# LayerNorm with GELU on one core: the last 128 rows as two half tiles, one of them on 15 DMA engines, and empty instructions ahead of two instruction streams

## The chip, the core and the metric

One NeuronCore of a Trainium2 chip. The metric is the device time of the whole kernel in microseconds (us). Every kernel below was run beside the kernel before on the same chip. "Span" is the time from the first to the last recorded instruction; the measured time of the same run is 1.8 to 2.0 us longer.

## The reference

```python
# x: (8, 1024, 2048) float32; gamma, beta: (2048,)
mean = np.mean(x, axis=-1, keepdims=True)
var = np.var(x, axis=-1, keepdims=True)
out = gamma * (x - mean) / np.sqrt(var + eps) + beta
return 0.5 * out * (1 + np.tanh(np.sqrt(2 / np.pi) * (out + 0.044715 * out ** 3)))
```

There are 8192 rows of 8 KB: 67.1 MB to read and 67.1 MB to write.

## The kernel before

The rows go through SBUF in 16 blocks of 512. A block is a tile of 128 partitions with 4 rows (32 KB) each, and there are 5 such slots. SyncE issues the loads, ScalarE the stores. A slot's next load waits until its store has landed.

```python
# SyncE
for b in range(B):
    s = slot(b)
    if stored(b):
        sy.wait_ge(s_store[s], stored(b))
    ...                                   # block 0: four loads of 1 MB, one for each q
    if b:
        sy.dma_start(out=xts[s], in_=xg[b]).then_inc(s_load[s], 16)
```

For each of the 64 tiles of 128 rows VectorE takes the statistics, GpSimd the power -1/2, ScalarE normalizes, VectorE multiplies by gamma, TensorE adds beta in PSUM by a matmul, and ScalarE applies GELU and issues the store: whole blocks, but the last block tile by tile.

```python
# ScalarE, after the GELU of tile q of block b
if by_row(b):                             # the last block
    ac.dma_start(out=og[b, :, q:q + 1], in_=xt[:, q:q + 1])._wait_ge(
        s_r, b + q + 1).then_inc(s_store[slot(b)], 16)
```

VectorE's stream is a prologue (block 0), a loop of 20 tiles that runs 3 times, and an end. ScalarE's stream is unrolled.

## Time and profile before

| | before |
|---|---|
| time, median of 6 runs | 319.69 us (319.23 to 320.06) |
| span of the profiled run | 317.8 us |
| DMA, mean over the span | 423 GB/s |
| busiest compute engine | VectorE, 83% |
| last store issued, last store landed | 305.32, 316.50 us |
| last packet of 14 DMA engines | 313.3 to 313.9 us |
| last packet of the other two | 316.06 us both |

The last two rows are not on the page. The trace holds a record of each DMA packet with queue, start, duration and size, but without its engine. The packets were strung into 16 chains, as the prediction tells, choosing the fit with the smallest sum of gaps; the last packet of each chain is the last of one engine. Two engines at the same point in time can swap names in it; a chain 2 us behind the rest cannot be mistaken. "Excess" is what a chain's data packets took beyond the usual duration of their size (1213 ns for 32 KB, 309 ns for 8 KB).

### The profile page before, as it was taken

What the parts mean: (1) busy time and instruction counts of PE and PEld (TensorE: products, weight loads), DVE (VectorE), ACT (ScalarE), POOL (GpSimd) and SP (SyncE); (2) the same over time, 40 slices, a digit from 0 to 9 for tenths busy, and PEclk for the clock granted to TensorE, in tenths of its full rate; (3) what the DMA queues carried; (4) which work ended last, traced back from release to release, by engine and by line L of the source; (5) the groups of instructions that cost most, each with busy time, mean ns of one, the idle gap of its engine ahead of it and who ended that gap; (6) DMA issues with size and microseconds to landing.
All of it is one profiled execution on the core that took longest, in us unless ns stands there. A gap on an engine that the chain in (4) does not pass through costs nothing.

```text
span 317.8 us, 2075 instructions
## 1 busy us (share of the span) xinstructions
PE 244.3 (77%) x520; PEld 57.1 (18%) x520; DVE 265.0 (83%) x514; ACT 253.9 (80%) x132; POOL 79.0 (25%) x73
## 2 busy tenths in 40 slices
PE   2769988888888898888877868598595895868810
PEld 1211222111212122211111111122121111112100
DVE  3499999999999999999969799696996969879500
ACT  2679999999999999999969779696995969968920
POOL 1033323232323231323213222231312213212000
DMA  7999999999999999999999999999999999999994
GB/s 291 438 462 396 459 396 445 412 454 404 458 400 459 422 437 445 412 450 408 458 417 441 437 421 454 404 458 412 450 433 425 450 408 450 408 458 421 437 404 206
DMA packets 5571, 134.27 MB, mean 423 GB/s; under 512 B 656, under 2 KB 704, under 8 KB 704
## 3 DMA queue, kind: packets, MB, share of 16 engines
q1 hardware_dynamic: 2736, 67.11, 49.4%
q10 hardware_dynamic: 2832, 67.13, 49.1%
q14 instruction: 3, 0.02, 0.0%
HBM read 67.13 MB, written 67.11 MB: 422 GB/s over the span
## 4 chain that ended last, share of the span: by engine, by line
DMA 44%; DVE 27%; ACT 19%; PE 3%; issue 2%; ACTq 1%; DVEq 0%; SPq 0%
DMA out_dram<-xt 27%; DVE sts L148 15%; DMA xt<-in_x_dram 15%; ACT yk L201 12%; DVE zg L164 9%; ACT xt L208 7%; PE ps L226 2%; DMA rows<-in_gamma_dram 2%; DVE mvs L157 2%; DVE nms L141 1%; ACTq L216 1%; DVE ves L158 1%; PE ps L243 1%; ACT g_t L197 1%; ACTq L211 0%
## 5 line engine op out<-in xcount | busy, mean ns | idle before, releaser
L148 DVE BATCH_NORM_STATS2 sts<-xt 128x6 f32<-128x512 f32 x256 | 163.5, 681 | 23.7 <-DMA xt<-in_x_dram 21.7
L201 ACT ACTIVATE yk<-xt,nms,rss 128x2048 bf16<-128x2048 f32 x64 | 134.1, 2095 | 41.7 <-DVE nms L141 41.2
L243 PE MATMUL ps<-zg,ident 128*128 128x512 bf16 x256 | 120.8, 627 | 50.9 <-DVE zg L164 50.9
L132 POOL TENSOR_TENSOR rss<-ves,mhalf 128x1 f32<-128x1 f32 x64 | 78.0, 1219 | 216.5 <-DVE ves L158 157.0
L239 PE MATMUL ps<-b_hl,ones_b 33*128 33x512 bf16 x256 | 120.6, 624 | 2.2 <-PEq L234 2.2
L208 ACT ACTIVATE xt<-ps 128x2048 f32<-128x2048 f32 x64 | 118.8, 1857 | 1.5 <-PE ps L243 1.5
L164 DVE TENSOR_TENSOR zg<-yk,g_t 128x2048 bf16<-128x2048 bf16 x64 | 78.0, 1218 | 5.0 <-ACT yk L201 3.0
L243 PEld LDWEIGHTS ps<-zg,ident 128*128 128x128 bf16 x256 | 27.6, 130 | 144.1 <-DVE zg L164 108.7
L239 PEld LDWEIGHTS ps<-b_hl,ones_b 33*128 33x128 bf16 x256 | 27.0, 127 | 92.1 <-issue 88.4
L157 DVE BATCH_NORM_AGGREGATE mvs<-sts 128x2 f32<-128x24 f32 x64 | 16.9, 264 | 2.2
L141 DVE TENSOR_SCALAR nms<-mvs,rss 128x1 f32<-128x1 f32 x64 | 12.6, 196 | 0.0
L226 PE MATMUL ps<-rows,ones 1*128 1x512 f32 x8 | 7.2, 1072 | 6.0 <-DMA rows<-in_gamma_dram 6.0
L158 DVE TENSOR_SCALAR ves<-mvs 128x1 f32<-128x1 f32 x64 | 9.8, 154 | 2.2
L194 ACT ACTIVATE b_hl<-rows 1x2048 bf16<-1x2048 f32 x1 | 1.9, 1909 | 4.9 <-DMA rows<-in_beta_dram 4.9
L226 PEld LDWEIGHTS ps<-rows,ones 1*128 1x128 f32 x8 | 2.5, 323 | 9.2 <-DMA rows<-in_gamma_dram 6.0
L172 DVE TENSOR_TENSOR b_hl<-rows,b_hl 1x2048 bf16<-1x2048 f32 x1 | 2.3, 2281 | 2.1 <-ACT b_hl L195 2.1
L197 ACT ACTIVATE g_t<-ps 128x2048 bf16<-128x2048 f32 x1 | 1.9, 1877 | 2.4 <-PE ps L226 2.4
L190 ACT ACT_TABLE_LOAD x1 | 1.3, 1283 | 0.9 <-SPq L106 0.9
L167 DVE MEMSET b_hl<- 33x1024 uint32 x1 | 0.9, 912 | 1.2 <-SPq L106 1.2
L195 ACT ACTIVATE b_hl<-rows 1x2048 bf16<-1x2048 f32 x1 | 1.9, 1908 | 0.0
L123 POOL MEMSET ones<- 65x128 f32 x1 | 0.2, 202 | 0.5 <-SPq L106 0.5
L127 POOL TENSOR_SCALAR_AFFINE_SELECT ident<-ident 128x128 bf16<-128x128 bf16 x1 | 0.3, 294 | 0.1
(7 smaller groups left out, 0.9 us busy)
## 6 DMA issues: line engine op xcount, KB each, us to landing
xt<-in_x_dram SPq DMA_DIRECT2D x15, 4096.0 KB, 24.3
out_dram<-xt ACTq DMA_DIRECT2D x15, 4096.0 KB, 37.0
xt<-in_x_dram SPq DMA_DIRECT2D x4, 1024.0 KB, 8.1
out_dram<-xt ACTq DMA_DIRECT2D x4, 1024.0 KB, 12.7
rows<-in_beta_dram ACTq DMA_DIRECT2D x2, 8.0 KB, 5.6
rows<-in_gamma_dram ACTq DMA_DIRECT2D x1, 8.0 KB, 5.0
```

The lines of the kernel that those rows point to most:

```text
L132: po.tensor_tensor(out=rss[:, c], in0=ves[:, c], in1=mhalf, op=ALU.pow)._wait_ge(s_a, k + 1).then_inc(s_q, 1)
L141: ve.tensor_scalar(out=nms[:, c], in0=mvs[:, q, 0:1], scalar1=rss[:, c], scalar2=-1.0, op0=ALU.mult, op1=ALU.mult)._wait_ge(s_q, count).th ...
L148: ins = ve.bn_stats(out=sts[:, q, j, :], in_=xr[:, j, :])
L157: ve.bn_aggr(out=mvs[:, q], in_=sts[:, q])._wait_ge(s_o, count + 1).then_inc(s_o, 1)
L158: ve.tensor_scalar(out=ves[:, q:q + 1], in0=mvs[:, q, 1:2], scalar1=float(eps), scalar2=1.0, op0=ALU.add, op1=ALU.mult)._wait_ge(s_o, coun ...
L164: ve.tensor_tensor(out=zgs[q % 2], in0=yks[q % 2], in1=g_t, op=ALU.mult)._wait_ge(s_n, count).then_inc(s_z, 1)
L197: ac.activation(out=g_t, in_=pss[0], func=ACT.Identity)._wait_ge(s_tg, 1).then_inc(s_c, 1)
L201: ac.activation(out=yks[t % 2], in_=xts[slot(b)][:, q], func=ACT.Identity, scale=rss[:, q:q + 1], bias=nms[:, q:q + 1])._wait_ge(s_p, t + ...
L208: ins = ac.activation(out=xt[:, q], in_=pss[i % 2], func=ACT.Gelu_apprx_tanh)._wait_ge(s_t, i + 1)
L226: ins = pe.matmul(pss[0][:, cols(j)], lhsT=ones[64:65], rhs=rows[64:65, j * K // nsub:(j + 1) * K // nsub, :d // K], start=True, stop=True)
L239: ins = pe.matmul(ps[:, cols(j)], lhsT=ones_b, rhs=b_hl[:, cols(j)], start=True, stop=False)
L243: ins = pe.matmul(ps[:, cols(j)], lhsT=ident, rhs=zgs[k % 2][:, cols(j)], start=False, stop=True)
```

## The change

The intent: the kernel is bound by its DMA engines, so it ends when the last of them has drained its queue. The change takes work from engine 15 and tries to move the engines' instruction fetches, which use DMA engines too. Of the last 128 rows, 64 become a half tile whose rows go 60 over 15 engines and 4 over 4 engines; the other 64 become a second half tile in a free slot, over all 16. VectorE and ScalarE run empty instructions first.

```diff
+H = 64
+E = 4
+PAD_DVE, PAD_ACT = 76, 68
...
+    def halves(v, a, h):
+        return [(v[n1:n1 + H - E], a[32:32 + H - E]), (v[n1 + H - E:n1 + H], a[0:4 * E:4]),
+                (v[n1 + H:n1 + 2 * H], h[32:32 + H])]
...
+                sy.dma_start(out=x_end[:, :R - 1], in_=last(xf)).then_inc(s_load[slot(B - 1)], 16)
+                for v, a in x_half[:2]:
+                    sy.dma_start(out=a, in_=v).then_inc(s_tail, 16)
+                sy.wait_ge(s_store[slot(B)], stored(B))
+                sy.dma_start(out=x_half[2][1], in_=x_half[2][0]).then_inc(s_load_h, 16)
...
                 ve.memset(b_hl, 0.0).then_inc(s_m, 1)
+                for _ in range(PAD_DVE):
+                    ve.nop()
...
+                for _ in range(PAD_ACT):
+                    ac.nop()
                 ac.wait_ge(s_m, 1)
```

Cut: the stores of the half tiles, which go the same way, and one more tile in each compute engine's stream.

## The prediction

> **What bounds the kernel now.** I read four things in this order: the page's busy shares and slices, the windows of the last 18 us, the end of the timeline, and last the trace's records of single DMA packets.
>
> The page first. No compute engine is over 83% busy, but the DMA row stands at 9 from the second slice to the last but one:
>
> ```profile
> PE 244.3 (77%) x520; PEld 57.1 (18%) x520; DVE 265.0 (83%) x514; ACT 253.9 (80%) x132; POOL 79.0 (25%) x73
> ...
> DMA  7999999999999999999999999999999999999994
> ...
> DMA packets 5571, 134.27 MB, mean 423 GB/s; under 512 B 656, under 2 KB 704, under 8 KB 704
> ...
> q14 instruction: 3, 0.02, 0.0%
> ```
>
> The bytes are fixed by the reference: 67.1 MB in, 67.1 MB out. Neither the change nor anything else in this design moves fewer. So the time is start-up (first data packet at 1.95 us), a stretch in which 16 DMA engines never rest, and the end. The queue 14 row is 3 fetches of instructions of 8 KB that use the same engines.
>
> The windows of the end (columns: busy us of PE, PEld, DVE, ACT, POOL with counts, clock, DMA share, GB/s):
>
> ```profile
> 306.00:312.00 6.00, 0.00 (x0) 0.00 (x0) 0.00 (x0) 0.00 (x0) 0.00 (x0) 1.00 1.01 425
> 312.00:314.00 2.00, 0.00 (x0) 0.00 (x0) 0.00 (x0) 0.00 (x0) 0.00 (x0) 1.00 0.74 311
> 314.00:318.00 4.00, 0.00 (x0) 0.00 (x0) 0.00 (x0) 0.00 (x0) 0.00 (x0) 1.00 0.06 25
> ```
>
> From 306 on nothing computes and the engines only drain. Between 312 and 314 they begin to run out, and after 314 just 6% of 16 engines works: two of them, by the next reading.
>
> The timeline of the end, to see whether compute feeds the drain in time:
>
> ```profile
> 280.06 0.69 DVE L148 BATCH_NORM_STATS2 sts<-xt 128x6 f32<-128x512 f32 x1 [2.57 <-DMA xt<-in_x_dram]
> ...
> 293.26 0.34 ACTq L211 DMA_DIRECT2D out_dram<-xt  x1
> ...
> 297.61 0.34 ACTq L211 DMA_DIRECT2D out_dram<-xt  x1
> ...
> 301.97 0.34 ACTq L211 DMA_DIRECT2D out_dram<-xt  x1
> ...
> 305.32 0.34 ACTq L211 DMA_DIRECT2D out_dram<-xt  x1
> ```
>
> The last store is issued at 305.32, yet lands 11.2 us later, at 316.50 (its 16 completions come from 313.71 to 316.50). By the same completions the store ahead of it was done on most engines at 311.5. So the last data were in the queue some 4 to 5 us before their turn: compute does not set the end.
>
> Last, the packets. In the trace each engine starts its next packet within a few ns of the end of the one before, and each takes 8 packets of each large transfer, so the records can be strung into 16 chains. I did that for the whole run. Fourteen chains end between 313.3 and 313.9 us. Two end at 316.06, 2.4 us late:
>
> - Chain A has no instruction fetch; from 45 us on its 32 KB packets take now and then some 33 ns more than the usual 1213 ns, 2.74 us in all. On most engines this excess is 0.
> - Chain B serves two of the instruction fetches, at 34.3 and 99.5 us (325 and 309 ns). The packet after each is stretched by 662 and 531 ns, one at 40.1 by some 0.4 us more than on other engines, and three later ones by 0.55 us. Together about 2.8 us, less a few tenths in which it is luckier than the rest.
> - A third chain serves the fetch at 109.9 us and ends at 313.9: 309 ns, and 245 ns on the packet after it.
>
> So the end is **two late DMA engines**. The span is 1.73 us more than their last packet (316.06 to 317.8), and the measured 319.67 is 1.87 more than the span.
>
> **What the Trainium skill says.** "DMA: Bandwidth & Descriptors", in "Why a DMA increments its semaphore by 16 and not by 1": a transfer uses the largest number of engines up to 16 that divides its slowest dimension, and these are the lowest-numbered. 60 rows therefore go to engines 0 to 14, four each, and 4 rows to engines 0 to 3; the 64 rows of the other half go to all 16. The trace of before has only transfers over 16 engines, so it neither shows nor denies this. The same page, "Where 436 GB/s comes from", has 435 GB/s for 16 engines; here 32768 bytes in 1213 ns are 27.0 GB/s for one and 432 for sixteen, which agrees. The same page, "Latency and other measured facts", says engines 7 and 15 are usually slower, from a cause tied to transfers that GpSimd issues. There are none here, and still one engine (A) is slow without a fetch. The records do not number the engines; that A is 15 is my inference. "Runtime: NRT & Kernel Launch", "Instruction fetch mechanics": an engine's sequencer fetches its next page by DMA while it runs, in 16 KiB blocks. The trace agrees on the fetching but shows packets of 8192 bytes, 128 instructions. The two fetches on B come when VectorE has run 54 and 184 recorded instructions, 130 apart, so I put B down to VectorE's stream; the third comes with ScalarE's 66th.
>
> **The change part by part.**
>
> *Bytes per engine.* Of the last tile's 128 rows, engine 15 loses four (8 KB each) in and four out: 64 KB, or 8 x 8192 bytes at 27.0 GB/s = 2.43 us. Engines 0 to 3 gain one row each way: 16 KB, 0.61 us. If A is engine 15 it ends at 316.06 - 2.43 = 313.6, level with the rest; engines 0 to 3 end at 313.9 to 314.5.
>
> *One more tile of compute.* A half tile costs as much time as a whole one, since time goes by columns. At the end one tile takes 4.35 us (293.26 to 297.61). But the last block's main load is now 3 MB instead of 4. Issued at 255.76, the old one took 24.2 us; three quarters of that is 18.1, so it lands near 274, before VectorE needs it at 277.5. The wait of 2.57 us goes. The last issue: 305.32 - 2.57 + 4.35 + 0.34 for one more transfer = 307.4. Its data's turn is near 312.4. Five us of slack, so this is hidden.
>
> *The half tile's load.* It waits for block 11's store, landed at 275.1, and is needed at 277.5 + 4 x 4.12 = 294. Hidden.
>
> *The empty instructions.* Sequencer instructions in a row on VectorE start 0.10 us apart (26.46, 26.56, 26.66) and on ScalarE about the same. So 76 take up to 7.6 us, from 1.3 to 8.9, and 68 on ScalarE 6.6 us, from 2.9 to 9.5. VectorE's first statistics move from 5.82 to 8.9; ScalarE's two bias rows from 7.05 to 9.5. The chain of set-up goes through the gamma matmuls (to 13.22) and ends at 15.13, so at most 0.5 us comes of it. The first store at 36.45 moves by that; the loads alone keep the engines busy until about 47 us (20 MB at 432 GB/s). Cost 0.
>
> *The fetches.* Pages follow the count of instructions, so VectorE's first crossing moves into its empty instructions (near 6 us), the second to what was its 108th (near 60 us), and ScalarE's first to near 8 us, with a second possible. The number hardly falls. What can fall is the stretching. If an early fetch costs 0.3 to 0.6 instead of the 1.4 us that the one at 34.3 cost with what followed, B ends at 315.0 to 315.3; if the other stretches go too, near 314.
>
> *Sum.* The end is the later of A and B: from 316.06 to 314.2 at best, to 315.2 in the middle, unchanged at worst. With 1.73 + 1.87 us behind it: 317.8, 318.8, or 319.7. I take 318.2, as the padding was surely put in for these fetches.
>
> **Rivals.** (1) *One laggard remains.* Lightening engine 15 frees only one of the two; if B keeps its 2.4 us the time stays at 319.3 to 319.7. For it: the same number of fetches. Against: the padding would then have no purpose. (2) *Engine 15 is B, or A is another one.* Then A, with no less to do, holds the end: 319.7, and if the late engine is among 0 to 3, 320.3. For it: the records show no engine numbers. (3) *The end turns compute-bound,* through one more tile: would need 5 us more than I count; then 320 or more. Against: the lost wait of 2.57 us. (4) *The padding delays the start:* needs 10 us of delay to reach the DMA. Unlikely.
>
> **Range and chances.** Full success 317.8 (some 45%), half 318.8 (30%), none 319.7 (20%), worse 5%. Range 317.2 to 319.9. The whole late stretch is 2.4 us, 0.8%, so 2% (6.4 us) can hardly be won; and a loss of 6 us would need a mechanism that I do not see. Faster 0.01, same 0.98, slower 0.01.
>
> **What would show it.** Right: completions of the last store within 1 us of each other instead of 2.8; chains of packets that end within 1 us; one chain with 64 KB less and four with 16 KB more; no wait before VectorE's first statistics of the last block; the last issue near 307.4. Wrong: one chain still ends 2 us after the rest (rival 1 or 2, told apart by whether it has fetches); the DMA share falling below 0.9 before 311 (rival 3); the lighter chain ending 2.4 us before all others (engine 15 was never late).

## The result, and the profile after

| | before | changed |
|---|---|---|
| time, median of 6 runs | 319.69 us | 319.71 us (319.63 to 319.9) |
| ratio | 1 | 1.0004 (0.9991 to 1.0016) |
| span of the profiled run | 317.8 us | 318.1 us |
| last packet, latest engine | 316.06 us | 316.37 us |

Nothing moved. The 1.5 us foretold did not come.

The windows of the end of the changed kernel (columns as in the prediction):

```profile
306.00:312.00 6.00, 0.00 (x0) 0.00 (x0) 0.00 (x0) 1.51 (x1) 0.00 (x0) 1.00 0.99 419
312.00:314.00 2.00, 0.00 (x0) 0.00 (x0) 0.00 (x0) 0.00 (x0) 0.00 (x0) 1.00 0.82 344
314.00:318.00 4.00, 0.00 (x0) 0.00 (x0) 0.00 (x0) 0.00 (x0) 0.00 (x0) 1.00 0.08 33
```

The engines are full until 312 and run out between 312 and 314, but 8% of 16 engines still works after 314, where it was 6%. The late stretch is still there. The timeline says that compute did not cause it (the `x2` is the two stores of the first half tile):

```profile
277.73 0.69 DVE L191 BATCH_NORM_STATS2 sts<-xt 128x6 f32<-128x512 f32 x1 [0.18 <-DMA xt<-in_x_dram]
...
299.61 0.34 ACTq L261 DMA_DIRECT2D out_dram<-xt  x1
...
303.95 1.56 ACTq L261 DMA_DIRECT2D out_dram<-xt  x2
...
307.55 0.59 ACTq L261 DMA_DIRECT2D out_dram<-xt  x1
```

VectorE's wait for the last block shrank from 2.57 to 0.18 us, and the last store is issued at 307.55, 4 to 5 us before its turn. As foretold, the extra tile is hidden.

The chains show what happened. In this kernel they partly bear numbers, since the byte counts differ: one chain has 64 KB less (engine 15), four have 16 KB more (engines 0 to 3).

| chain | last packet, before | last packet, changed |
|---|---|---|
| engine 15 | in the group at 313.3 to 313.9 | **311.42** |
| A: late, no instruction fetch | 316.06 | **316.37** (one of engines 4 to 14) |
| B: late, two fetches | 316.06 | 315.60 (one of 0 to 3) |
| C: one fetch | 313.91 | 314.86 (one of 0 to 3) |
| the other ten of 4 to 14 | 313.3 to 313.9 | 313.6 to 313.9 |

The chain that was relieved had not been late; it now ends 2.1 us before the earliest of the rest. This reading needs no engine numbers: the chain is known by its 64 KB less. The chain that was late kept all its work.

The second part of the change left no mark at all. VectorE's first statistics, in the kernel before and in the changed one:

```profile
5.82 2.47 DVE L148 BATCH_NORM_STATS2 sts<-xt 128x6 f32<-128x512 f32 x4 [3.68 <-DMA xt<-in_x_dram]
```

```profile
5.76 2.47 DVE L191 BATCH_NORM_STATS2 sts<-xt 128x6 f32<-128x512 f32 x4 [3.62 <-DMA xt<-in_x_dram]
```

76 instructions ahead of it cost no time, and the three fetches come at 34.4, 99.7 and 109.0 us, as before (34.3, 99.5, 109.9). The program that each kernel builds to says why: VectorE has 38 instructions ahead of its loop in both, with no empty one among them. They were dropped when the program was built.

### The profile page after: what moved, and what is told of

Read it like the earlier page. It is cut to its first block, busy times and chain, and to the rows that moved or that the text cites. A ratio compares the mean times of both kernels' runs of the same rounds, so it can differ in the third digit from the quotient of the medians.

```text
span 318.1 us, 2115 instructions
## 1 busy us (share of the span) xinstructions
PE 248.0 (78%) x528; PEld 58.0 (18%) x528; DVE 269.2 (85%) x522; ACT 257.8 (81%) x134; POOL 79.6 (25%) x74
## 4 chain that ended last, share of the span: by engine, by line
DMA 43%; DVE 27%; ACT 21%; PE 2%; issue 2%; ACTq 2%; DVEq 0%; SPq 0%
DMA out_dram<-xt 26%; DVE sts L191 15%; DMA xt<-in_x_dram 15%; ACT yk L251 13%; ACT xt L256 8%; DVE zg L207 8%; PE ps L274 2%; DMA rows<-in_gamma_dram 2%; ACTq L261 2%; DVE mvs L200 2%; DVE nms L184 1%; DVE ves L201 1%; ACT g_t L246 1%; ACTq L265 0%; DVEq L223 0%
## 5 line engine op out<-in xcount | busy, mean ns | idle before, releaser
L191 DVE BATCH_NORM_STATS2 sts<-xt 128x6 f32<-128x512 f32 x260 | 165.9, 680 | 21.4 <-DMA xt<-in_x_dram 19.2
L251 ACT ACTIVATE yk<-xt,nms,rss 128x2048 bf16<-128x2048 f32 x65 | 136.1, 2093 | 39.9 <-DVE nms L184 39.4
L291 PE MATMUL ps<-zg,ident 128*128 128x512 bf16 x260 | 122.7, 627 | 49.1 <-DVE zg L207 49.1
L287 PE MATMUL ps<-b_hl,ones_b 33*128 33x512 bf16 x260 | 122.5, 624 | 2.2 <-PEq L282 2.2
L256 ACT ACTIVATE xt<-ps 128x2048 f32<-128x2048 f32 x65 | 120.7, 1857 | 1.7 <-PE ps L291 1.7
L207 DVE TENSOR_TENSOR zg<-yk,g_t 128x2048 bf16<-128x2048 bf16 x65 | 79.2, 1219 | 5.0 <-ACT yk L251 3.1
## 6 DMA issues: line engine op xcount, KB each, us to landing
xt<-in_x_dram SPq DMA_DIRECT2D x1, 3072.0 KB, 22.3
```

What stands on the lines that cost most here:

```text
L191: ins = ve.bn_stats(out=sts[:, q, j, :], in_=xr[:, j, :])
L207: ve.tensor_tensor(out=zgs[q % 2], in0=yks[q % 2], in1=g_t, op=ALU.mult)._wait_ge(s_n, count).then_inc(s_z, 1)
L251: ac.activation(out=yks[t % 2], in_=tiles[t], func=ACT.Identity, scale=rss[:, c], bias=nms[:, c])._wait_ge(s_p, t + 1).then_inc(s_n, 1)
L256: ins = ac.activation(out=tiles[i], in_=pss[i % 2], func=ACT.Gelu_apprx_tanh)._wait_ge(s_t, i + 1)
L287: ins = pe.matmul(ps[:, cols(j)], lhsT=ones_b, rhs=b_hl[:, cols(j)], start=True, stop=False)
L291: ins = pe.matmul(ps[:, cols(j)], lhsT=ident, rhs=zg[:, cols(j)], start=False, stop=True)
```

## The experiments

**Theory 1**: the span is the last packet of the latest DMA engine and some 1.7 us; that engine is not 15, and the padding does not exist. **Rivals**: A is engine 15 after all; the fetches alone make both late; the extra tile takes back what the dealing out gives; the end hangs on something other than the latest engine.

### Which engine is late

The kernel before, with the last tile's load in nested pieces, so that each engine gets its own number of 8 KB packets:

```diff
+COUNTS = [*range(15, 0, -1), 8]
...
+                for k in COUNTS:
+                    sy.dma_start(out=xts[s][p0:p0 + k, R - 1], in_=xg[b, p0:p0 + k, R - 1]).then_inc(s_tail, 16)
+                    p0 += k
```

> The kernel before, but the last tile's load is cut into 16 transfers of 15, 14, ... 1 and 8 rows. If a transfer of k rows goes to the k lowest engines, each engine then has its own number of 8 KB packets in the end (16 rows for engine 0, 9 for engine 7, none for engine 15) and the chains of packets get numbers. Theory 1: the chain without a fetch that is late (A) is not engine 15 but engine 7, and the two chains with instruction fetches (B with two, C with one) are among engines 0 to 3. Rival: A is engine 15, and the changed kernel's run only looked otherwise; then the chain with no row of the last tile's load carries the small excess of 2 us and more. The time is about that before, up to 322, because engine 0 gets 8 rows (2.4 us) more.

Measured: 329.07 us in a single look (16 small loads come late, and VectorE waits 19.18 us for the last tile; so my "up to 322" was wrong, but the time is not the point here). The 16 chains have 16 different counts, 0 to 7 and 9 to 16, just what nested sets of engines give. That the smallest sets are the lowest numbers is the page's statement that the prediction cites; the records have no numbers to test it. A has 12 rows: **engine 4**. B has 13: **engine 3**. C has 15: **engine 1**. Engine 15, with no row, has an excess of 0.05 us between 45 and 280 us, against 2.26 us for A. That the late chain would be engine 7 was wrong too; that it is not 15 is shown.

### What makes engine 4 late

The loads and stores with no compute (a wrong result). Block 0's load and the last block's store are here one transfer of 4 MB each, not four of 1 MB, and gamma and beta are not loaded:

```diff
... (all streams of compute are taken out)
             @block.scalar
             def _(ac):
+                for b in range(B):
+                    s = slot(b)
+                    n_l = 16 * sum(slot(c) == s for c in range(b + 1))
+                    ac.wait_ge(s_load[s], n_l)
+                    ac.dma_start(out=og[b], in_=xts[s]).then_inc(s_store[s], 16)
```

> Wrong result on purpose: the loads and stores of the kernel before with no compute (x is copied). If the small excess of chain A (2.7 us over the run, from 45 us on) comes from the DMA engine itself, one chain still ends some 2 us late with no fetch on it. If it comes from what the compute engines do, all chains without fetches end within 0.5 us of each other. The instruction streams are short, so no fetch of instructions is expected within the run, and no chain B. Time near 312 to 317.

Measured: 317.23 us (one look), just above the 317 expected. The windows of its end, where only GpSimd's column is left of the engines:

```profile
306.00:312.00 6.00, 0.00 (x0) 1.00 1.00 431
312.00:314.00 2.00, 0.00 (x0) 1.00 0.61 262
314.00:318.00 4.00, 0.00 (x0) 1.00 0.00 0
```

Nothing works after 314: all 16 chains end between 313.2 and 313.8, with no fetch and no late chain. So both late chains come with the compute and its instructions, not from the engines themselves. With this even end the last packet comes at 313.81 instead of 316.06, 2.2 us earlier, and the single look is 2.5 us below the kernel before.

Next, the same copy with 3000 memsets of one element on VectorE beside it:

```diff
+            @block.vector
+            def _(ve):
+                with ve.Fori(0, 60):
+                    for k in range(50):
+                        ins = ve.memset(ones[0:1, k:k + 1], 0.0)
+                    ins.then_inc(s_a, 1)
+                    ve.wait_ge(s_a, 1)
+                    ve.sem_inc(s_a, -1)
```

> Wrong result on purpose: loads and stores with no compute, as in the copy alone, plus 3000 memsets of one element on VectorE beside them. If the small excess of chain A comes with the number of instructions that engines run (about 2000 in the kernel before for 2.7 us), one chain now ends 2 to 4 us after the rest, as none did in the copy alone. If it comes with the data that compute reads and writes, all chains end within 0.6 us of each other again, near 313.5.

Measured: 320.50 us (one look). Fifteen chains end between 314.5 and 314.7 and one at 316.80. That one has an excess of 3.0 us from 30 us on, nearly all before VectorE is done at 113 us, for instructions that touch next to no data. Then the kernel before without the matmuls that add beta (wrong):

```diff
-                            ins = pe.matmul(ps[:, cols(j)], lhsT=ones_b, rhs=b_hl[:, cols(j)], start=True, stop=False)
...
-                                            start=False, stop=True)
+                                            start=True, stop=True)
```

> Wrong result on purpose: the kernel before without the matmuls that add beta, so 512 of its 2075 recorded instructions are gone, and no transfer is changed. If chain A's small excess goes with the number of instructions, it falls from 2.74 us by about a quarter, to 2.0 or 2.1, and A ends near 315.4, while B stays at 316.0, so the time hardly moves. If it goes with something else (bytes, the stores themselves), A stays at 316.0.

Measured: 319.10 us (one look). The first line of the page, before and here:

```profile
span 317.8 us, 2075 instructions
```

```profile
span 317.3 us, 1627 instructions
```

The instructions fall to 0.78 of their number. A's excess from 45 us on falls from 2.74 to 2.08 us, 0.76 of it, and A ends at 315.57. B happened to end at 315.55 here, where 316.0 was expected, and the time followed, 0.6 us below before. That the fall is not chance can be read from the other traces: the 32 KB packets after 45 us that took 5 to 60 ns longer than usual sum to 2.4 to 3.0 us over all chains in ten kernels with the full compute (the first attempt with GpSimd, below, is left out, as its packets are slow until 48 us), to 1.93 without beta's matmuls and to 0.13 in the copy alone. So A's excess goes with the **number of instructions run**. Divided by the instructions recorded in the same stretch it is near 1.5 ns each in the full kernel (2.74 us over 1788) and without beta (2.08 over 1388), and 1.2 ns in the copy with memsets (3.0 over 2430). Whether the running or the recording of them puts this traffic on engine 4 stays open: every run here was recorded.

### Padding that stays

The kernel before with the padding alone. Waits that are already met take the place of the empty instructions; two of them merge into one instruction in the build, so twice as many are written:

```diff
                 ve.memset(b_hl, 0.0).then_inc(s_m, 1)
+                for _ in range(152):
+                    ve.wait_ge(s_m, 1)
...
+                for _ in range(136):
+                    ac.wait_ge(s_m, 1)
                 ac.wait_ge(s_m, 1)
```

> The kernel before with the padding alone, by waits that are already met instead of empty instructions, so that 76 and 68 instructions really stand in the program. Theory 1 (the padding was dropped when the program was built, and A holds the end anyway): the fetches move from 34 and 99 us to about 6 and 60 us on B, from 109 to about 8 us on C, with perhaps one more; B's end may fall, but A stays at 316.0, so the time stays within 0.3 us of before. Rival (the fetches set the end for both late chains): 1 us or more faster.

Measured: 319.78 us, ratio 1.0002 (0.9985 to 1.0019). VectorE's first statistics show that this padding is real:

```profile
10.02 2.47 DVE L148 BATCH_NORM_STATS2 sts<-xt 128x6 f32<-128x512 f32 x4 [7.88 <-issue]
```

The fetches moved to 12.2 and 66.2 us on B and 10.7 us on C, where a second one came at 217.6. They moved, but their number rose from 3 to 4 (the page's line of queue 14, which carries the fetches, before and here):

```profile
q14 instruction: 3, 0.02, 0.0%
```

```profile
q14 instruction: 4, 0.03, 0.0%
```

B ended at 315.61, C at 315.07, and A at 316.53, which held the time.

The changed kernel with the same padding:

> The changed kernel with padding that stays in the program (waits already met). Theory 1: A, at 316.4 in the changed kernel, still holds the end, so within 0.3 us of the kernel before. Rival (the change as meant, with engine 15 late and the fetches moved): 1.5 to 2 us faster, near 317.8.

Measured: 319.88 us, ratio 1.0008 (0.9991 to 1.0025). A ends at 316.17, B at 315.59, C at 316.35 (its second fetch, and the 16 KB more that engine 1 got from the dealing out), engine 15 at 311.29. So the change as it was meant gives nothing either: it relieves the wrong engine, and gives more to two of those that carry the fetches.

### The half tiles alone

```diff
-        return [(v[n1:n1 + H - E], a[32:32 + H - E]), (v[n1 + H - E:n1 + H], a[0:4 * E:4]),
+        return [(v[n1:n1 + H], a[32:32 + H]), None,
                 (v[n1 + H:n1 + 2 * H], h[32:32 + H])]
```

> The changed kernel, but the first half tile's 64 rows go over all 16 engines in one transfer each way: the half tiles alone, without the dealing out. Theory 1: every engine has the bytes that it had before, engine 15 ends level with the rest near 313.5 instead of 311.4, and A and B at 315.6 to 316.4 set the end: the time is that of before and of the changed kernel within 0.3 us. Rival (the dealing out does give something, which the extra tile of compute takes back): slower than before by 1 us or more.

Measured: 319.79 us, ratio 0.9999 (0.9983 to 1.0016). Fourteen chains end between 313.4 and 314.1, A at 316.33, B at 316.35. The extra tile costs nothing, so it takes nothing back: the last rival but one falls.

### More work for some engines

The kernel before with two needless loads near 275 us over the lowest EX engines:

```diff
+                sy.dma_start(out=free[0:EX], in_=xg[0, 0:EX]).then_inc(s_x, 16)
+                sy.dma_start(out=free[16:16 + EX, :2], in_=xg[0, 16:16 + EX, :2]).then_inc(s_x, 16)
```

With EX = 3:

> The kernel before plus two needless loads near 275 us, over the 3 lowest engines alone: 32 KB and 16 KB for each of them, 1.82 us of work each by the packet times (1213 and half of it). Theory 1 (the end is set by engines 3 and 4, which end 2.4 us after the rest; engines 0 to 2 have slack): the three end near 315.4 to 315.7, so the time stays within 0.3 us of before. Rival (all engines matter alike, or the end is set by something else than the last engine): 1.8 us times 3/16, 0.3 us, or 1.8 us slower.

Measured: 321.10 us, ratio 1.0045 (1.0029 to 1.006). A miss in time, 1.4 us where I expected 0.3 at most. The chains say why: the three engines did not end by 315.7 but at 315.85, 317.42 and 317.47. On two of them the extra 32 KB packet took 2.4 us, not 1.2, and the packets after it were stretched too. I had put the rows into partitions 0 to 2. The Trainium skill, "SBUF — State Buffer", "Door 1: The DMA port swizzle", has such neighbours on one port; three engines then write through one. This run agrees, and the test was spoilt by it as a test of slack.

With EX = 5, engines 0 to 4:

> The same needless loads over the 5 lowest engines, 0 to 4, so that the two late chains get 1.82 us more as well. Theory 1: 1.8 us slower than before, near 321.5 (0.6%). Rival: no slower than the same loads over 3 engines, or only by 0.2 us.

Measured: 321.50 us, ratio 1.0053 (1.0038 to 1.0069), as expected in size, but the same clash of ports is in it (B at 319.47, A at 318.42 in the profiled run, which is the slowest of the four, 322.92). Read together, the two do not tell the engines apart. They do show that the time follows whichever engine is last.

### Attempts to relieve the right engines

As the nested sets above show, a plain transfer of few rows takes some engines always and others never, so it cannot leave out 3 and 4 alone. I tried with transfers that GpSimd issues, in two ways. First, in block 1's load:

```diff
+                        for p0, p1 in ((0, 96), (96, 99), (99, 102)):
+                            sy.dma_start(out=xts[s][p0:p1], in_=xg[b, p0:p1]).then_inc(s_load[s], 16)
...
+                po.dma_start(out=x1[102:124], in_=xg[1, 102:124]).then_inc(s_sw, 16)
```

> The kernel before, with block 1's load dealt out so that engines 3 and 4 get 64 KB (2.43 us) less of it: 96 partitions over all 16, 2 x 3 over engines 0 to 2, and the rest by transfers that GpSimd issues, 22 partitions over 11 engines and 4 more over 8. If these go to consecutive engines that follow on from those of the transfer before (a small one of 5 rows first), the 11 are engines 5 to 15 and the 8 are engines 5 to 12, 0.6 us more each. Theory 1: the chains then end between 313.3 and 314.4, and the time falls by 1.5 to 2 us, to near 318. Rival (the way that GpSimd's transfers are dealt out is another, or their making costs more than they give): no faster than before.

Measured: 345.50 us, ratio 1.0807 (1.0789 to 1.0824). Its page:

```profile
GB/s 270 163 223 213 225 194 432 435 442 431 431 431 431 427 424 436 439 435 439 431 431 431 435 427 427 435 439 435 439 431 435 435 431 427 427 439 347 374 389 244
```

From the second to the sixth slice, 9 to 52 us, the engines move half of what they did, and until 48 us a 32 KB packet takes around 2.4 us. 96 partitions over 16 engines are 6 each, which do not match the groups of 4 that share a port, so I take it for the same clash. The GpSimd transfers came in the same run, but their last data packet ends at 21.8 us; from then until 48 us only SyncE's loads are in flight, and the packets are still slow. So the GpSimd transfers do not hold that stretch; that the ports do is argued, not shown.

Second, with each row kept on its port where possible, on the changed kernel's first half tile. Small extra transfers between GpSimd's were meant to shift the engines that its next one takes (not shown):

```diff
+        low = [(v[n1 + 44 + 3 * j:n1 + 47 + 3 * j], a[32 + j:44:4]) for j in range(4)]
+        pool = [(v[n1:n1 + 44], a[52:96]), None, (v[n1 + 56:n1 + 59], a[20:32:4]), (v[n1 + 59:n1 + 64], a[96:116:4])]
```

> The changed kernel without the padding, its first half tile dealt out so that engines 3 and 4, not 15, get nothing of it: 12 rows over engines 0 to 2 by four small transfers from SyncE and ScalarE, 44 rows by GpSimd over 11 engines, meant as 5 to 15, and the last 8 rows by GpSimd over 5 to 12; each row in a partition that its engine also serves in the full transfers. [...] Engines 3 and 4 lose 64 KB, 2.43 us each. Theory 1 (these two set the end): all chains end between 313.3 and 314.6, 1.5 to 2 us faster than before, near 318.0. Rival (GpSimd's transfers cost more than they give, or are dealt out in another way): no faster, or slower as in the first attempt.

Measured: 322.64 us, ratio 1.0089 (1.0074 to 1.0105). Two assumptions failed. GpSimd's 44 rows went over 15 engines (15, 15 and 14 packets of 8 KB in three turns), not over 11. And ScalarE needed 4.03 us to issue four small stores, which held back its last GELU:

```profile
306.16 4.03 ACTq L289 DMA_DIRECT2D out_dram<-xt  x4
...
310.32 1.88 ACT L284 ACTIVATE xt<-ps 128x2048 f32<-128x2048 f32 x1 [4.19 <-issue]
312.23 0.58 ACTq L289 DMA_DIRECT2D out_dram<-xt  x1
```

The last store is issued at 312.23, after its turn: here the end did become bound by compute and issue.

> A control: the same kernel and the same number of transfers from GpSimd, but its round of engines is moved on so that the 44 rows fall on engines 0 to 10, engines 3 and 4 among them, which lose nothing. Theory 1: the late engines stay late and the time is that of before or up to 1 us more. Rival (the gain of the run with the skip comes from having GpSimd issue transfers, whichever engines serve them): as fast as that run.

Measured: 322.65 us, ratio 1.009 (1.0074 to 1.0105), the same as the run it was to control. As neither dealt the rows out as meant, the pair says nothing for or against Theory 1. No version here beats the kernel before.

### The last packet and the span

| kernel | last packet | span | difference |
|---|---|---|---|
| copy alone | 313.81 | 315.45 | 1.64 |
| without beta's matmuls | 315.57 | 317.31 | 1.74 |
| before | 316.06 | 317.80 | 1.74 |
| half tiles alone | 316.35 | 318.05 | 1.70 |
| changed with padding that stays | 316.35 | 317.90 | 1.55 |
| changed | 316.37 | 318.07 | 1.70 |
| before with padding | 316.53 | 318.27 | 1.74 |
| copy with memsets | 316.80 | 318.72 | 1.92 |
| extra work for 3 engines | 317.47 | 319.13 | 1.66 |
| extra work for 5 engines | 319.47 | 321.13 | 1.66 |
| last load in pieces | 325.57 | 327.27 | 1.70 |
| second attempt with GpSimd, and its control | 318.29, 318.32 | 320.75, 320.78 | 2.46 both |
| first attempt with GpSimd | 341.66 | 343.71 | 2.05 |

In the eleven kernels whose transfers come from SyncE and ScalarE alone the last packet moves by 11.8 us and the difference by 0.4 us. The three with transfers from GpSimd lie above all of these (2.05 and 2.46 us), and no run says why. This carries Theory 1's first half: the end is the latest engine, whichever it is.

## Why the prediction was right or wrong

- **The bound**: right. DMA engines that never rest, then two late ones; the span follows the latest packet.
- **"If A is engine 15 it ends at 316.06 - 2.43 = 313.6"**: this step failed. The saving was sized well (engine 15 ends 2.1 us before the earliest of the ten that kept their bytes, for 2.43 foretold), but it fell on an engine that was not late: A, at 316.06 before, is engine 4 and ends at 316.37. The prediction had named this outcome as a sign of being wrong ("the lighter chain ending 2.4 us before all others"). The prediction had said that the records do not number the engines, and then leant on the diff, whose author aimed at 15, and on a page's remark about engines 7 and 15. A diff tells what its author believed.
- **"76 take up to 7.6 us"** and **"VectorE's first crossing moves into its empty instructions"**: failed, since the instructions were not in the program. Waits in their place did take time, 10.02 against 5.82 us for the first statistics (8.9 foretold), and did move the fetches. "The number hardly falls" was right and too mild: it rose by one.
- **"the padding was surely put in for these fetches"**: an intent was taken for an effect. On this I put 75% on a gain. Rivals 1 and 2, to which I gave 20%, are both what happened: A was another engine, and the fetches stayed.
- **The extra tile**: right. It costs as much as a whole one (260 statistics of one form at 680 ns on the changed page, 256 at 681 ns before). Last issue 307.4 foretold, 307.55 measured; the wait before the last block fell to 0.18 us. The load of 3 MB was mis-sized, 22.3 us to landing and not 18.1, without consequence.
- **Engines 0 to 3**: right within 0.2 us for the two without fetches (314.24 and 314.66, for 313.9 to 314.5). B ended at 315.60 though it got 0.61 us more work and its fetches had not moved, so that it came near the 315.0 to 315.3 foretold is luck; its excess from 30 us on was 1.5 us where it had been 2.8. Over the runs that excess varies by more than a microsecond, and what stretches those packets stays open.
- **The range** (317.2 to 319.9) holds 319.71; the predicted 318.2 is off by 1.5 us. The 1.87 us from span to time pairs the span of one run with the median of several; the profiled run took 319.58 us, 1.78 more than its span. The slip of 0.1 us changes nothing.

What is shown: the latest engine sets the end; engine 15 was not late; the empty instructions were dropped when the program was built; the half tiles are hidden; the change gives nothing even with padding that stays; A's excess goes with the count of instructions. The number 4 for A rests on the page's rule that a transfer of k rows takes the lowest k engines; that A is not the engine relieved does not. What is only argued: that relieving engines 3 and 4 would gain 2 us. No run did it.

## What to carry to other kernels

When the DMA engines are full to the end, ask which of them ends last, and number it before dealing work around: a load in nested pieces of 15, 14, ... rows gives each engine its own count in one run. Check in the trace or in the built program that padding is there at all; an edit that leaves every time stamp in place probably never reached the chip. When a change aims at one of two late things, the other sets the time.

## What the Trainium skill lacked or had wrong

- "DMA: Bandwidth & Descriptors", "Latency and other measured facts", names engines 7 and 15 as usually slower, with a guessed cause that is tied to GpSimd's transfers, of which this kernel has none. Here engine 15 is not slower (0.05 us of excess between 45 and 280 us); engines 3 and 4 end some 2.4 us late, 3 with two instruction fetches and 4 with an excess of 1.2 to 1.5 ns for each instruction recorded. No page has the latter.
- "Runtime: NRT & Kernel Launch", "Instruction fetch mechanics", has blocks of 16 KiB and calls the cost of a crossing mostly hidden. Here a fetch is one packet of 8192 bytes for about 128 instructions, on engine 3 for one engine's stream and engine 1 for another's. With the packets stretched after it, a fetch costs its DMA engine 0.55 to 1.0 us, which delays all its later packets when the DMA engines never rest. No page tells which DMA engine serves which stream.
- "DMA: Bandwidth & Descriptors", "Why a DMA increments its semaphore by 16 and not by 1": that a plain transfer of k rows goes to k engines, the smaller sets lying in the larger ones, is borne out for k from 1 to 15 by 16 different row counts. Of the two rules that it has for GpSimd's transfers, the exception held: 44 rows went over 15 engines, three each and two on the last, not four each over 11.
- No page that I read says that empty instructions are dropped when a program is built: 76 and 68 were written, none was in the program.
- No page that I read has the cost of issuing small stores one after another: four of 24 KB took ScalarE 4.03 us (0.74 to 1.29 us each), where one of 1 MB takes 0.34 us.
